# Row factors broadcast by way of DRAM, one gate behind a bank copy, and another order of VectorE's last steps

## The chip, the cores and the metric

The kernel runs on one core of a Trainium2 chip. Such a core has five engines with instruction queues of their own: TensorE (PE), which multiplies matrices; VectorE (DVE); ScalarE (ACT); GpSimd (POOL); and SyncE (SP), which here only issues transfers. Sixteen DMA engines move data between DRAM and the core's memory (SBUF); ACT, POOL and SP can issue transfers from their queues. PE writes its results to eight accumulation banks (PSUM) of 128 x 512 numbers of 32 bits, from which ACT and VectorE read them. Each engine works through its queue in order, and engines wait for one another through semaphores.

The metric is the device time of one execution in microseconds. The median of some runs is compared between two kernels; a profile comes from one more execution.

## The reference

One decoder layer on 1,024 tokens of width 1,024, in 32-bit floating point: a token mixer of two head groups (gated linear attention, GLA, and sliding-window attention), cross-attention into 256 memory tokens, and a gated MLP with a causal convolution of width 3. Each part begins with an RMS norm, and one more ends the layer.

```python
def rms_norm(x, g):
    xf = x.astype(jnp.float32)
    y = xf * lax.rsqrt(jnp.mean(xf * xf, axis=-1, keepdims=True) + EPS)
    return (y * g.astype(jnp.float32)).astype(x.dtype)

def conv_ffn(h, w_up, conv_w, conv_b, w_down):
    u = h @ w_up
    u = lax.conv_general_dilated(u, conv_w[:, None, :].astype(u.dtype), window_strides=(1,),
                                 padding=[(CONV_WIDTH - 1, 0)],
                                 dimension_numbers=('NWC', 'WIO', 'NWC'),
                                 feature_group_count=2 * D_FF) + conv_b
    gate, val = jnp.split(u, 2, axis=-1)
    return (jax.nn.silu(gate) * val) @ w_down
...
        hn = rms_norm(h, norm_mix[l])
        proj = hn @ w_in[l]
        gq, gk, gv, gr, ga, sq, sk, sv = jnp.split(proj, split_at, axis=-1)
...
        h = h + conv_ffn(rms_norm(h, norm_ffn[l]), w_up[l], conv_w[l], conv_b[l], w_down[l])
    return rms_norm(h, norm_final)
```

`D_FF` is 2,816, so the up projection has 5,632 columns: 22 column blocks of 128 for the gate and 22 for the values.

## The kernel before

**Products.** Every operand of a large product is split into a high part in a rounded 32-bit format (`float32r`), made by ACT, and a low part, made by VectorE as source less high part (`split`, lines 106 to 116; weights by way of `load`, line 118, from a staging buffer `st` into `w`). One product is three matmuls: high by high, high by low, low by high (`mm3`, line 147). PE's time is mostly these matmuls of 128 x 128 by 128 x 512.

**Order of the work.** A planner takes the program as written, models the time of each instruction, and fixes each engine's queue before the kernel runs. Inside `manual_schedule` the named engines keep the order of the program text among the instructions written there; others may be placed between them. `issue_after` and `add_manual_dep` with `NoSync` add an edge that only fixes which of two instructions of one engine is issued first. Waits for data are added by the framework. A pool's tag with `bufs=n` is a ring of n buffers; the banks are such rings too (`F`, `S`, `O`, `T`).

**The first stage, rows_a (line 467).** Eight row tiles of `x` (128 tokens each) are loaded. For each, PE transposes it (line 520), ACT and VectorE split the transposed tile into `xh` and `xl`, and PE multiplies it with 272 columns of `w_in`. PE, VectorE and ACT are in manual order. After each odd row tile, `factors` makes the sums of squares of two tiles on ACT (line 197) and their factors 1/rms by steps of two columns on ACT and VectorE (lines 183 to 191), into two columns of `rstd`, tile `rstd_x`, [128, 8]. `evac` scales the two results with them: `ga` on ACT (line 477), then two results on VectorE (line 479), of which `sv` goes to DRAM by POOL (`sv_d`, line 481) after every fourth tile.

Later products have the tokens along the free axis, so they need the factors as a row that stands in all 128 partitions: `rstd_bc`, tile `rbx`, [128, 1024]. `broadcast_rows` (line 199) makes it: for each half four matmuls of 128 columns of the factors, stretched along the free axis, by the identity (line 205; each shows as two instructions), into a bank of role `O`, and a copy by ACT (line 207). The call stands behind the manual block, so the planner places it.

**What follows it.** `vectors` brings gains into columns, by a transpose on PE; `swa_bias` makes the masks of the sliding window by way of two DRAM tiles (`line`, `skew`); `gla_gates` transposes `ga` (tile `prob`, line 676). `cols_swa` makes `sk` and then four tiles `sq`: for each half of the tokens 24 matmuls into one of the two `F` banks, and VectorE's `self.column` (line 610) multiplies bank and `rbx`. `save_x` writes `x` back to DRAM by VectorE sums (line 438) and POOL's queue (`xt_d`, line 439). Then the softmax of the sliding window runs on VectorE and ACT beside the column products of GLA on PE (`swa`, line 1008).

**The up projection (lines 1765 to 1904).** Column block j of the gate and block j of the values make a pair. Pairs 0 and 1 are done plainly (`up_plain`). Pair 2 is `up_first` and the others are `up_winograd`: seven block products `p1`, `p4`, `p6`, `p7` and so on instead of eight, with sums of weights (`t1` to `t4`, made by VectorE) and of activations (`s1` to `s4`); VectorE and ACT add the banks together. In `up_first`, `p5` is one of three `F` banks: the product of `t1` and `s1` is copied by ACT to `s5` (line 1853, tile `o`), and then PE adds the product of `b22` and `s4` to the same bank, so PE must wait for the copy.

`ffn_up(j)` (line 1896) finishes a pair: `conv` for both halves (one step on ACT, line 1890, and two on VectorE, line 1892, each), the Silu of the gate on ACT (line 1901), the product on VectorE (line 1902), and the write to DRAM by POOL. In `run`, `ffn_up(1)` stands between the parts of `up_first` (line 2288), and the code behind it is the second half of `up_first`.

**The end (lines 2163 to 2201).** The last product of the down projection ends with row tile 3 in manual order: its 512 columns come in two halves of 256 in two banks (`last_half`, line 2163). For each half VectorE adds the bank to `c12[3]` (line 2172), and ACT sums the squares (line 197). From the sums come the row factors (`partly`, line 2045; `guess`, lines 2048 to 2051; `newton`, lines 2055 and 2059), and `finish` scales two halves of the row tile: `one` on ACT (line 2065), `two` on VectorE (line 2070), each with a write to the output. Tile 2's `two` (`rows[i - 1][1]`) stands between the two halves of tile 3.

Of the kernel before, what the change touches and what calls it, by code (L numbers as in the profile page):

```python
# [28 lines left out]
P = 128  # L29
# [32 lines left out]
class Layer:  # L62
# [404 lines left out]
    def rows_a(self, keep, new):  # L467
# [40 lines left out]
        ssq = self.small("ssq", [P, NT], bufs=1)  # L508
        self.rstd = self.const.tile([P, NT], F32, name="rstd_x")
        self.rstd_bc = self.bc_tile("rbx")  # L510
        xh, xl = (self.xnew("x" + s, (P, NK, T), F32R) for s in "hl")
        self.x = [(xh[:, k], xl[:, k]) for k in range(NK)]
        self.xact = self.whole(self.x)
# [20 lines left out]
        with self.tc.manual_schedule(engines={e.PE, e.DVE, e.Activation}):  # L534
            transposed(0, 0)
            split_weights(st[0], 0, 3)
            transposed(0, 4)
            for i in range(NT):
                ps = self.bank("FO"[i % 2])
                cuts = (0, 3, 6, NK) if i == 0 else (0, NK)  # L540
                for k0, k1 in zip(cuts, cuts[1:]):
                    if i == 0 and k0:
                        split_weights(st[k0 // 3], k0, k1)
                    if i < NT - 1 and k1 == cuts[-1 if i == 0 else 1]:
                        transposed(i + 1, 0)
                        transposed(i + 1, 4)
                    products(ps, i, range(k0, k1))
                if i % 2:
                    for q in (i - 1, i):
                        factors(q)  # L550
                    evac(i - 1, done)
                    evac(i, ps)
                done = ps
        self.broadcast_rows(self.rstd, self.rstd_bc)

    def rows_b(self, new, weights, between):

# [1273 lines left out]
    def up_first(self, weights, new):  # L1831
# [18 lines left out]
        tt(out=u3, in0=p7, in1=u2, op=ALU.add)  # L1850
        tt(out=ug[:, t1s], in0=p4, in1=u3, op=ALU.subtract)
        product(p5, t1, s1, True)
        nc.scalar.copy(out=s5, in_=p5)  # L1853
        tt(out=uv[:, t1s], in0=s5, in1=u3, op=ALU.add)
        product(p5, b22, s4, False)
        tt(out=uv[:, t0], in0=p5, in1=u2, op=ALU.add)
# [39 lines left out]
    def ffn_up(self, j, us, new):  # L1896
# [1 line left out]
        nc = self.nc  # L1898
        yg = self.conv(us[0], j, new)
        yv = self.conv(us[1], NJ + j, new)  # L1900
        last = nc.scalar.activation(out=yg, in_=yg, func=AF.Silu)
        self.gated = nc.vector.tensor_tensor(out=yg, in0=yg, in1=yv, op=ALU.mult)
        nc.gpsimd.dma_start(out=self.g_d[j], in_=yg)
        return last
# [38 lines left out]
    def ffn_down(self, pre, hcnew):  # L1943
# [232 lines left out]
        def end(bank, ops):  # L2176
            with self.tc.manual_schedule(engines={mybir.EngineType.PE, mybir.EngineType.DVE,
# [7 lines left out]
                for i in range(4):  # L2185
                    _, (_, guess, newton, *partly) = factors[i]
                    if i < 3:
                        half_row(y[i], c12[i], i, 1)()
                    else:
                        read[0]()  # L2190
                    if i:
                        rows[i - 1][1]()
                    if i == 3:
                        partly[0]()
                        read[1]()
                    guess()
                    newton()
                    rows[i][0]()
# [134 lines left out]
```

## Time and profile before

| | us |
|---|---|
| median of 3 runs | 1272.4 |
| lowest and highest run | 1268.08, 1274.22 |
| the profiled execution | 1267.25 |
| its span, first to last instruction | 1265.5 |

The profile shows the profiled execution. In the timeline each row has the start in us from the span's start, the time, the engine, the line of the kernel, the operation, the tiles written and read (numbers of buffers left out), how many instructions were merged, and in brackets the idle time of the engine ahead of it and what ended that. `SPq`, `ACTq` and `POOLq` are queues that issue transfers. Matmuls are pipelined and their ends are modelled, so the distance from one start to the next says more than a duration. Some tiles carry the name of the buffer that they share: the second half of `up_first` writes into tiles called `o` and `uy`.

```profile
q1 hardware_dynamic: 173750, 121.51, 32.3%
q0 software_dynamic: 17184, 52.08, 12.7%
q10 hardware_dynamic: 160, 0.27, 0.1%
L207 ACT COPY rbx<-psO x2: 581/586/590, 41.9 to 45.7; 128x512 f32<-128x512 f32 x2
L191 DVE TENSOR_TENSOR rstd_x<-rs_y,rs_t x4: 151/160/161, 19.4 to 44.8; 128x2 f32<-128x2 f32 x4
```

The first three rows are DMA queues with packets, megabytes and the share of the sixteen engines' time: q1 is filled by SP, q0 by POOL, q10 by ACT. The last two are from the views of the tiles `rbx` and `rstd_x`: the shortest, median and longest time in ns, and the first and last start. The last factors are made at 44.8 us, and the second half of the broadcast row is copied at 45.7.

### The profile page before, as it was taken

The numbers are of one execution on the slowest core, as the hardware profiler recorded it, in microseconds if no ns is written. First come the engines' busy times: TensorE is split into PE (matmuls) and PEld (weight loads), VectorE is DVE, ScalarE is ACT, GpSimd is POOL, SyncE is SP. The second block draws the span as 40 slices with busy tenths as digits, with TensorE's granted clock in tenths as the row PEclk, the third lists the DMA queues.
The fourth block names the chain that finished last, engine by engine and source line by source line (L and its number), as shares of the span: only waits on it lengthen the run. The fifth ranks groups of instructions, "written<-read, shape, count | busy, mean of one in ns | idle before, by whom it ended". The sixth has DMA issues, their size and how long they took to land.

```text
span 1265.5 us, 19111 instructions
## 1 busy us (share of the span) xinstructions
PE 1249.9 (99%) x7303; PEld 1047.7 (83%) x7303; DVE 1005.9 (79%) x1697; ACT 632.2 (50%) x1167; POOL 124.4 (10%) x216
## 2 busy tenths in 40 slices
PE   8999999999999999999999999999999999999997
PEld 8887778989888889888887888888888888888886
DVE  6846886478556967897798989899888777999687
ACT  5426577246544535853566434434434435454455
POOL 1310332101221000000040000000000000000001
PEclk9999999999999999999999999999999999999999
DMA  7651355358643446153474335655622348610204
GB/s 229 201 154 51 85 135 139 121 183 272 208 150 115 139 150 223 44 180 129 141 133 126 100 109 141 150 124 140 185 83 68 100 149 326 227 64 10 74 24 152
DMA packets 191186, 175.08 MB, mean 138 GB/s; under 512 B 66689, under 2 KB 150838, under 8 KB 191094
## 3 DMA queue, kind: packets, MB, share of 16 engines
q1 hardware_dynamic: 173750, 121.51, 32.3%
q0 software_dynamic: 17184, 52.08, 12.7%
q8 instruction: 57, 0.93, 0.3%
q14 instruction: 35, 0.29, 0.1%
q10 hardware_dynamic: 160, 0.27, 0.1%
HBM read 121.64 MB, written 49.29 MB: 135 GB/s over the span
## 4 chain that ended last, share of the span: by engine, by line
PE 85%; DVE 8%; ACT 3%; DMA 2%; issue 1%; POOL 0%; SPq 0%; ACTq 0%; DVEq 0%; POOLq 0%
PE psS L1828 15%; PE psF L1828 14%; PE psF L1978 6%; PE psS L1978 6%; PE psF L1346 5%; PE psF L149 5%; PE psF L150 5%; PE psF L151 5%; PE psS L1623 3%; PE psO L1978 2%; PE psT L1978 2%; PE psS L149 2%; PE psS L150 2%; PE psS L151 2%; PE psF L1623 2%; ACT prob L1089 1%
## 5 line engine op out<-in xcount | busy, mean ns | idle before, releaser
L110 ACT CAST w<-st 128x1024 fp32r<-128x1024 f32 (+1 forms) x147 | 125.7, 858 | 187.4 <-PE psS L1978 39.9
L111 DVE TENSOR_TENSOR w<-st,w 128x1024 fp32r<-128x1024 f32 (+1 forms) x147 | 143.5, 978 | 48.9 <-ACT w L110 48.7
L1892 DVE SCALAR_TENSOR_TENSOR uy<-uy,vec,uy 128x1023 f32<-128x1023 f32 (+1 forms) x88 | 112.1, 1280 | 2.0 <-ACT uy L1890 0.4
L1828 PE MATMUL psS<-a,w 128*128 128x512 f32 x384 | 92.4, 389 | 0.0
L1978 PE MATMUL psF<-w,w 128*128 128x512 f32 x318 | 88.9, 389 | 0.0
L1978 PE MATMUL psS<-w,w 128*128 128x512 f32 x312 | 87.4, 389 | 0.0
L1828 PEld LDWEIGHTS psS<-a,w 128*128 128x128 f32 x384 | 72.1, 188 | 15.0
L149 PE MATMUL psF<-xh,w 128*128 128x512 f32 x208 | 83.1, 400 | 0.0
L150 PE MATMUL psF<-xl,w 128*128 128x512 f32 x208 | 81.6, 392 | 0.0
L151 PE MATMUL psF<-xh,w 128*128 128x512 f32 x208 | 81.2, 390 | 0.0
L1828 PE MATMUL psF<-a,w 128*128 128x512 f32 x336 | 80.7, 389 | 0.0
L1828 PEld LDWEIGHTS psF<-a,w 128*128 128x128 f32 x336 | 63.1, 188 | 13.1
L1978 PEld LDWEIGHTS psF<-w,w 128*128 128x128 f32 x318 | 59.7, 188 | 12.4
L1890 ACT ACTIVATE uy<-uy,vec 128x1024 f32<-128x1024 f32 x44 | 54.8, 1246 | 29.8 <-DVE uy L1883 26.5
L1978 PEld LDWEIGHTS psS<-w,w 128*128 128x128 f32 x312 | 58.6, 188 | 12.1
L1828 PE MATMUL psS<-act,wx 128*128 128x512 f32 x252 | 60.5, 389 | 0.0
L1828 PE MATMUL psF<-act,w 128*128 128x512 f32 x240 | 57.8, 390 | 1.4 <-ACT o L1853 1.4
L1828 PE MATMUL psS<-act,w 128*128 128x512 f32 x240 | 58.0, 389 | 0.0
L1828 PEld LDWEIGHTS psS<-act,wx 128*128 128x128 f32 x252 | 47.3, 188 | 9.8
L1089 ACT ACTIVATE prob<-prob,nm 128x256 f32<-128x256 f32 (+1 forms) x64 | 30.8, 482 | 48.6 <-DVE nm L1085 48.6
L1828 PE MATMUL psF<-act,wx 128*128 128x512 f32 x228 | 54.8, 389 | 0.0
L1828 PEld LDWEIGHTS psF<-act,w 128*128 128x128 f32 x240 | 45.0, 188 | 11.1 <-ACT o L1853 1.8
(582 smaller groups left out, 3101.1 us busy)
## 6 DMA issues: line engine op xcount, KB each, us to landing
st<-in_w_up_dram SPq DMA_DIRECT2D x44, 512.0 KB, 3.8
g_d<-uy POOLq DMA_DIRECT2D x22, 512.0 KB, 3.0
act<-in_w_down_dram SPq DMA_DIRECT2D x12, 512.0 KB, 9.1
st<-g_d SPq DMA_DIRECT2D x10, 512.0 KB, 3.2
res<-g_d SPq DMA_DIRECT2D x10, 512.0 KB, 10.7
st<-in_w_in_dram SPq DMA_DIRECT2D x9, 512.0 KB, 6.2
ow_d<-pts POOLq DMA_DIRECT2D x32, 128.0 KB, 3.5
st<-in_w_v_c_dram SPq DMA_DIRECT2D x8, 512.0 KB, 6.6
```

The source lines that it names most:

```text
L110: h = nc.scalar.copy(out=hi, in_=src)
L111: l = nc.vector.tensor_tensor(out=lo, in0=src, in1=hi.bitcast(F32), op=ALU.subtract)
L149: mm(out, lhsT=lh, rhs=rh, start=start, stop=False, skip_group_check=joined)
L150: mm(out, lhsT=lh, rhs=rl, start=False, stop=False, skip_group_check=joined)
L151: mm(out, lhsT=ll, rhs=rh, start=False, stop=stop, skip_group_check=joined)
L1089: last = nc.scalar.activation(out=prob[:, n, :nk], in_=prob[:, n, :nk], func=AF.Exp, bias=nm[:, n:n + 1], accum_out=den[:, n:n + 1])
L1346: mm(ps[n], lhsT=left[n][l][:, q], rhs=self.qa[right[n]][q][r], start=new and q == 0 and i == 0, stop=new and q == 3 and i == 2, skip_grou ...
L1623: mm(ps, lhsT=left[n][l][:, q], rhs=right[n][q][r], start=new and q == 0 and i == 0, stop=new and q == 3 and i == 2, skip_group_check=not new)
L1828: self.nc.tensor.matmul(ps, lhsT=b[l][:, q], rhs=a[q][r], start=first and q == 0 and n == 0, stop=first and q == 3 and n == 2, skip_group_ ...
L1890: nc.scalar.activation(out=y, in_=u, func=AF.Identity, scale=self.v("cw2", j), bias=self.v("conv_b", j))
L1892: nc.vector.scalar_tensor_tensor(out=y[:, s:], in0=u[:, :T - s], scalar=self.v(nm, j), in1=y[:, s:], op0=ALU.mult, op1=ALU.add)
L1978: nc.tensor.matmul(ps[i], lhsT=g[:, l, tk], rhs=w[:, r], start=first and k == 0 and m == 0, stop=first and k == n - 1 and m == 2, skip_gro ...
```

## The change

Three edits.

1. The call of `broadcast_rows` for the first factors is gone. After every fourth row tile, behind `evac` and inside the manual block, ACT's queue writes four columns of the factors to a small DRAM tile (`rstd_d`, in the order of the tokens), and POOL's queue reads the 512 numbers back into all 128 partitions of `rbx`. The other call of `broadcast_rows` stays.
2. In `up_first`, the copy of the bank to `s5` is to be issued on ACT ahead of the Silu that `ffn_up(1)` has written earlier. The edge sets an order on ACT and no wait.
3. At the end, the second half of row tile 3 is read from its bank, and its squares are summed, ahead of the scaling of row tile 2 on VectorE, and not behind it.

```diff
@@ -508,6 +508,7 @@
         ssq = self.small("ssq", [P, NT], bufs=1)
         self.rstd = self.const.tile([P, NT], F32, name="rstd_x")
         self.rstd_bc = self.bc_tile("rbx")
+        rstd_d = self.dram.tile([2, 4, P], F32, name="rstd_d")
         xh, xl = (self.xnew("x" + s, (P, NK, T), F32R) for s in "hl")
@@ -550,8 +551,12 @@
                         factors(q)
                     evac(i - 1, done)
                     evac(i, ps)
+                if i % 4 == 3:
+                    h = i // 4
+                    nc.scalar.dma_start(out=rstd_d[h].rearrange("i p -> p i"), in_=self.rstd[:, 4 * h:4 * h + 4])
+                    nc.gpsimd.dma_start(out=self.rstd_bc[:, 512 * h:512 * h + 512],
+                                        in_=rstd_d[h].rearrange("(o i) p -> o (i p)", o=1).to_broadcast([P, 512]))
                 done = ps
-        self.broadcast_rows(self.rstd, self.rstd_bc)
@@ -1850,7 +1855,10 @@
         product(p5, t1, s1, True)
-        nc.scalar.copy(out=s5, in_=p5)
+        read = nc.scalar.copy(out=s5, in_=p5)
+        self.tc.add_manual_dep(self.silu.ins, read.ins.name,
+                               mybir.DependencyInfo(mybir.DependencyClass.NoSync, mybir.DependencyReason.DATA),
+                               reason="the bank is read ahead of the gate")
         tt(out=uv[:, t1s], in0=s5, in1=u3, op=ALU.add)
@@ -1898,7 +1906,7 @@
-        last = nc.scalar.activation(out=yg, in_=yg, func=AF.Silu)
+        last = self.silu = nc.scalar.activation(out=yg, in_=yg, func=AF.Silu)
         self.gated = nc.vector.tensor_tensor(out=yg, in0=yg, in1=yv, op=ALU.mult)
@@ -2188,11 +2196,12 @@
                     else:
                         read[0]()
+                    if i == 3:
+                        read[1]()
                     if i:
                         rows[i - 1][1]()
                     if i == 3:
                         partly[0]()
-                        read[1]()
                     guess()
                     newton()
```

## The prediction

> **What bounds the kernel now.** I read the page's busy table first, then the busy time by stretch, then the DMA issues, and the timeline at the three places that the change touches.
>
> ```profile
> PE 1249.9 (99%) x7303; PEld 1047.7 (83%) x7303; DVE 1005.9 (79%) x1697; ACT 632.2 (50%) x1167; POOL 124.4 (10%) x216
> PE 85%; DVE 8%; ACT 3%; DMA 2%; issue 1%; POOL 0%; SPq 0%; ACTq 0%; DVEq 0%; POOLq 0%
> 128.00:160.00 32.00, 31.63 (x413) 24.82 (x402) 28.10 (x68) 18.87 (x53) 10.00 (x16) 1.00 0.35 85
> 690.00:705.00 15.00, 15.00 (x67) 12.41 (x67) 14.88 (x18) 7.18 (x9) 0.56 (x1) 1.00 0.41 125
> 1250.00:1265.50 15.50, 7.71 (x46) 6.69 (x44) 7.84 (x26) 7.60 (x22) 1.62 (x3) 0.90 0.36 135
> ```
>
> TensorE (PE) is busy for 99% of the span and makes 85% of the chain that ended last. In the rows of stretches the figures after the length are the busy time of PE, its weight loads, VectorE (DVE), ScalarE (ACT) and GpSimd (POOL). So a microsecond saved counts in full where it shortens PE's queue, or where it lies behind PE's last matmul, as in the last 15.5 us. It counts in part where another engine is as full as PE: VectorE has 14.88 of 15.00 us between 690 and 705, and 28.10 of 32.00 between 128 and 160. Each of the three edits falls under one of these.
>
> **Edit 1, the broadcast.** Before, PE copies the row factors to all partitions.
>
> ```profile
> 40.49 1.05 PE L205 MATMUL psO<-ident,rstd_x 128*128 128x128 f32 x8
> 41.30 0.48 PE L149 MATMUL psF<-xh,w 128*128 128x512 f32 x1
> ...
> 42.55 0.66 PE L205 MATMUL psO<-ident,rstd_x 128*128 128x128 f32 x4
> 42.97 0.48 PE L151 MATMUL psF<-xh,w 128*128 128x512 f32 x1
> 43.28 0.40 PE L149 MATMUL psF<-xh,w 128*128 128x512 f32 x1
> ...
> 44.98 0.71 PE L205 MATMUL psO<-ident,rstd_x 128*128 128x128 f32 x4
> 45.45 0.48 PE L150 MATMUL psF<-xl,w 128*128 128x512 f32 x1
> ```
>
> Durations overlap, so I count from start to start. The 16 instructions (two for each call) hold PE from 40.49 to 41.30, 42.55 to 42.97 and 44.98 to 45.45: 0.81 + 0.42 + 0.47 = 1.70 us. The first long matmul after a broadcast lasts 0.48 where the next lasts 0.40: 0.08 more, three times, 0.24. Removed from PE: 1.70 + 0.24 = 1.9 us. ACT also loses its two copies out of the bank, worth nothing, since PE doesn't wait for ACT in this stretch.
>
> Added are two DMAs per half of the rows: ACT's queue writes 512 numbers, each a piece of 4 bytes, and POOL's queue, which waits for that write, reads them back to all partitions (256 KB). The first half:
>
> ```profile
> 27.68 1.08 ACT L110 CAST xh<-psS 128x512 fp32r<-128x512 f32 x2
> 29.42 1.27 DVE L111 TENSOR_TENSOR xl<-psS,xh 128x512 fp32r<-128x512 f32 x2
> 50.15 0.68 DVE L610 SCALAR_TENSOR_TENSOR sk<-psF,rbx 128x512 f32<-128x512 f32 x1
> 1261.71 0.39 ACTq L2071 DMA_DIRECT2D out_dram<-c  x1
> ```
>
> ACT can issue its write at 27.68 and the factors are first used at 50.15: 22 us cover two DMAs. The issue (ACT's last one took 0.39) delays the casts queued behind it, but their reader on VectorE starts only at 29.42, so it hides. The second half is the tight one:
>
> ```profile
> 45.13 0.27 ACT L477 ACTIVATE ga<-psO,rstd_x 128x16 f32<-128x16 f32 x1
> 55.52 0.69 DVE L610 SCALAR_TENSOR_TENSOR sk<-psF,rbx 128x512 f32<-128x512 f32 x1
> 58.02 0.29 DVE L670 TENSOR_TENSOR prob<-ga,prob 128x128 fp32r<-128x128 f32 x1
> 59.34 1.03 PE L676 MATMUL psS<-ident,prob 128*96 128x128 f32 x8
> ke_d<-ke SPq DMA_DIRECT2D x8, 128.0 KB, 3.5
> mem_d<-st SPq DMA_DIRECT2D x8, 128.0 KB, 5.6
> res<-xt_d POOLq DMA_DIRECT2D x16, 256.0 KB, 3.2
> out_dram<-c SPq DMA_DIRECT2D x4, 256.0 KB, 2.2
> rel<-in_rel_bias_dram SPq DMA_DIRECT2D x1, 1.0 KB, 8.3
> 90.00:95.00 5.00, 5.00 (x24) 4.14 (x23) 0.69 (x1) 0.00 (x0) 0.00 (x0) 1.00 0.00 0
> ```
>
> The last figure of a DMA row is the time from issue to landing. ACT can issue behind `ga`, at 45.4. No row shows a write of 4-byte pieces; the bounds are the shortest and longest of these medians, 2.2 and 8.3, for each of the two DMAs in turn, so the second half is there between 45.4 + 4.4 = 49.8 and 45.4 + 16.6 = 62.0. I take the writes of 128-byte pieces, 3.5 to 5.6, middle 4.5, and the POOL read of the same size, 3.2: 53.1 us. When is that too late? PE would reach the end of `sk` at 55.5 - 1.9 = 53.6, so VectorE does not wait at all. If it waited, everything behind it would: from the second `sk` (55.52) to the end of `prob` (58.31) VectorE needs 2.8 us, and PE's transposes of `prob`, now due at 59.34 - 1.9 = 57.4, need that. So the limit is 57.4 - 2.8 = 54.6 us. With 53.1 the 1.9 us stay. Behind POOL's waiting DMA are the saves `xt_d`, `sv_d` and `line`. The longest chain from them leads over `line` to the masks of the softmax, and it has landed before 90: from there to 95 the DMA engines are empty (last row), and the scores come later still. That covers a delay of 5 us and more.
>
> The Trainium skill, "DMA: Bandwidth & Descriptors", section Specifications, says that pieces under 512 B make a DMA engine read, modify and write, which speaks against the 4-byte write; the same page, section Anatomy of one DMA, gives about 2.0 us plus bytes over 436 GB/s for each DMA. By that fit, an estimate, the pair would take 2.0 + 2.6 = 4.6 us and be there at 50.0, and the sum would be the same. No run here shows the 4-byte write.
>
> Does a saving at 45 us last? Up to 129 us the chain of work is PE. From 129 to 235 it is made of VectorE and ACT pieces, with PE filled by other products; those pieces start from PE's results at 129 and move with them. I let all of it pass, and keep 0 as the other end.
>
> **Edit 2, the gate.** The Silu of the second plain pair stands on ACT ahead of the copy for which PE waits.
>
> ```profile
> 679.05 2.88 PE L1828 MATMUL psF<-act,w 128*128 128x512 f32 x12
> 681.77 1.98 PE L1828 MATMUL psS<-a,w 128*128 128x512 f32 x8
> 685.16 3.01 PE L1828 MATMUL psF<-act,w 128*128 128x512 f32 x12 [1.42 <-ACT o L1853]
> 683.09 1.06 ACT L1901 ACTIVATE uy<-uy 128x1024 f32<-128x1024 f32 x1 [1.58 <-DVE uy L1892]
> 684.52 0.59 ACT L1853 COPY o<-psF 128x512 f32<-128x512 f32 x1
> 691.59 0.56 ACT L1871 COPY c<-psS 128x512 f32<-128x512 f32 x1
> 692.55 2.88 PE L1828 MATMUL psS<-a,w 128*128 128x512 f32 x12
> 695.30 0.68 DVE L1873 TENSOR_TENSOR c<-psS,c 128x512 f32<-128x512 f32 x1
> 696.63 2.88 PE L1828 MATMUL psS<-act,wx 128*128 128x512 f32 x12
> ```
>
> The bank is full at 679.05 + 2.88 = 681.93, ACT idles 1.58 us ahead of 683.09, and so the copy can end near 682.6 without holding up the Silu, which waits for VectorE anyway. PE's eight early matmuls end their turn at 681.77 + 8 x 0.227 = 683.58, and the next product starts there and not at 685.16: 1.6 us. What is late next? ACT's copy of the next pair ends at 692.15, and PE's use follows at 692.55, only 0.4 us later; VectorE's read of the next bank ends at 695.98, and PE overwrites at 696.63, 0.65 later. ACT and VectorE are tied to VectorE's full queue and don't come earlier by themselves. In the present order only 0.4 us would be left. But eight more matmuls of the pair's own `t1` product (1.8 us) wait behind these, and the planner fills such holes with them, as it did at 681.77. With all of them drawn ahead, the overwrite would be due at 696.63 + 0.45 - 1.6 = 695.5 (two of `t1` stand behind it now), so it starts at 695.98: 0.5 of the 1.6 lost, 1.1 left. I take 1.1; the ends are 0.4 and 1.6.
>
> **Edit 3, the end.** Nothing is added; one read moves ahead of a scaling.
>
> ```profile
> 1256.83 0.88 PE L2168 MATMUL psO<-pre,pre 128*128 128x256 f32 x6
> 1257.72 0.74 DVE L2070 SCALAR_TENSOR_TENSOR c<-c,ffac,nfin 128x512 f32<-128x512 f32 x1
> 1258.43 0.19 ACT L197 ACTIVATION_READ_ACCUMULATOR junk<-c 128x1 f32 x1
> 1258.73 0.42 DVE L2172 TENSOR_TENSOR c<-psO,c 128x256 f32<-128x256 f32 x1
> 1259.24 0.42 ACT L197 ACTIVATE junk<-c 128x256 bf16<-128x256 f32 x1 [0.62 <-DVE c L2172]
> ```
>
> PE's last matmul ends at 1257.71, so the second read can start at 1257.75 and not at 1258.73, and ends at 1258.17. Its sum of squares on ACT is then held by the first one, which ends at 1258.62; it starts at 1258.65 and not at 1259.24: 0.6 us. The scaling that moves back (0.74) ends near 1258.8, before the factors are needed (1259.2), and its output on POOL's queue leaves 0.4 us later, still far ahead of the last one. All that follows to the end hangs on this chain, so 0.6 us counts, between 0.5 and 0.6.
>
> **Sum.** 1.9 + 1.1 + 0.6 = 3.6 us, 0.3%. The profiled execution took 1267.25 us (span 1265.5), so it would become 1263.7. The median of the runs shown is 1272.4, 5 us above it, and its runs spread over 6 us; the forecast for the median is 1272.4 - 3.6 = 1268.8. About 0.5% (6.4 us) is what a measurement of this kernel can tell from no change.
>
> **Rivals.**
>
> First, *the first saving is lost*: the factors land near the point at which VectorE's wait eats it (54.6 + 1.9 = 56.5 us), or VectorE, 88% full between 128 and 160, holds PE there. For it: two DMAs in a row, and VectorE's fill. Against it: PE itself is busy for 31.63 of those 32 us. Left: 1.1 + 0.6 = 1.7; 1270.7.
>
> Second, *slower: the second half of the factors is late*. VectorE stands at `sk`, and the transposes of `prob` and all of PE behind them wait. Its price against before is the landing time less 56.5; it decides from there on, and at the upper bound of 62.0 it is 5.5. Less the 1.7 of the other edits: 3.8 slower, 1276.2. For it: writes of 4-byte pieces have no row, and the longest small DMA here took 8.3. Against it: that needs both DMAs at nearly the longest time.
>
> Third, *the gate's edge doesn't do what it says*: the copy still follows other ACT work, or the planner's new order gives back the 1.6. Then 1.9 + 0.6 = 2.5; 1269.9.
>
> **How the numbers follow.** Forecast 0.5, first rival 0.2, second 0.1, third 0.2. Forecast and rivals one and three all lie within 0.5%; only scatter of the medians, or a planner's order that happens to be much better, brings over 0.5%. Ends of the range: all ends at their best (1.9 + 1.6 + 0.6 = 4.1) against the lowest run, 1268.08, gives 1264.0; the highest run, 1274.22, with nothing gained, 1274.2. Chances: faster 0.15, within 0.5% 0.79, slower 0.06.
>
> **What would show it.** Right: no `L205` matmul on `rstd_x`; the second `sk` on VectorE near 53.6, with no wait for a DMA; the transposes of `prob` near 57.4; 129 to 235 passed 1.9 us earlier; no wait of PE for the copy into `o` at 685, and the next pair's work 2.5 to 3.5 us earlier in all at 705; 0.6 us less from PE's last matmul to the end. Wrong: a wait of VectorE on `rbx`, a new PE wait between 55 and 65 or 690 and 705, or another order of matmuls with waits of its own.

## The result, and the profile after

| | before | after |
|---|---|---|
| median, us (6 runs each) | 1268.17 | 1279.62 |
| lowest and highest run, us | 1267.64, 1274.22 | 1276.78, 1282.91 |
| profiled execution, us | 1267.25 | 1282.78 |
| its span, us | 1265.5 | 1281.1 |

The ratio is 1.008, with a 95% interval of 1.0051 to 1.0108: the changed kernel is slower by some 10 us (6.5 to 13.7; the two medians lie 11.5 apart), where the forecast said 3.6 us faster and the range ended at 1274.2. Three of the six runs before are those of the table ahead of the prediction; with the three others the median before fell from 1272.4 to 1268.17. From line 555 on, the lines of the changed kernel stand 5 lines further down than before, in the up projection and at the end up to 8.

The busy table and the chain of the changed kernel show hardly a difference:

```profile
PE 1254.8 (98%) x7287; PEld 1050.5 (82%) x7287; DVE 1006.2 (79%) x1697; ACT 631.5 (49%) x1165; POOL 125.7 (10%) x218
```

PE's sixteen broadcast instructions are gone (7303 became 7287), and yet PE is busy for 5 us longer, in a span that is 15.6 us longer. So PE both waits more and works more slowly. Its waits between 40 and 110 us say where (waiter, releaser, then the sum, the times and the longest, in us); before, this view shows no wait there:

```profile
PE psS L681 <- DVE prob L675: 4.8, 1, 4.8
PE psS L692 <- DVE prob L682: 2.6, 1, 2.6
PE psF L149 <- DVE sk L615: 1.3, 1, 1.3
```

All three hang on VectorE. VectorE's timeline in the same stretch shows what held it, and that it was not `rbx`; first a row of before, then rows of after:

```profile
47.20 1.21 DVE L123 TENSOR_TENSOR st<-st,vec 128x1024 f32<-128x1024 f32 x1
```

```profile
52.45 1.23 DVE L123 TENSOR_TENSOR st<-st,vec 128x1024 f32<-128x1024 f32 x1 [6.12 <-DMA st<-in_w_in_dram]
...
58.81 0.68 DVE L615 SCALAR_TENSOR_TENSOR sk<-psF,rbx 128x512 f32<-128x512 f32 x1
...
67.23 1.23 DVE L438 TENSOR_TENSOR gk<-xh,xl 128x1024 f32<-128x1024 f32 x1 [4.05 <-DMA xt_d<-gk]
```

VectorE waits 6.12 us for a load of weights that the change doesn't touch (before, the same instruction starts at 47.20 without a wait), and 4.05 us for a save (`xt_d`). The second product with `rbx`, at 58.81, waits for nothing. The DMA issues between 38 and 60 us, with the median time to landing at the end of each row, first before and then after:

```profile
st<-in_w_in_dram SPq DMA_DIRECT2D x4, 256.0 KB, 4.9
st<-in_w_in_dram SPq DMA_DIRECT2D x1, 512.0 KB, 7.4
```

```profile
st<-in_w_in_dram SPq DMA_DIRECT2D x4, 256.0 KB, 11.8
st<-in_w_in_dram SPq DMA_DIRECT2D x1, 512.0 KB, 12.5
rstd_d<-rstd_x ACTq DMA_DIRECT2D x1, 2.0 KB, 11.7
```

The new write of 2 KB lands after 11.7 us, and loads that share nothing with it but the DMA engines and DRAM take about twice their time. The stretches show the same from the side of the bytes (the last two figures are GB/s and, ahead of it, the time that packets took as a share of the sixteen engines' time, which here passes 1), again before and after:

```profile
46.00:50.00 4.00, 4.00 (x18) 2.27 (x16) 3.11 (x9) 0.32 (x1) 2.37 (x5) 1.00 1.22 277
```

```profile
46.00:50.00 4.00, 4.00 (x18) 3.29 (x18) 0.23 (x2) 0.00 (x0) 0.00 (x0) 1.00 2.16 69
62.00:66.00 4.00, 2.68 (x11) 2.34 (x11) 1.17 (x2) 0.00 (x0) 1.43 (x3) 0.50 0.96 366
66.00:70.00 4.00, 1.41 (x4) 0.80 (x3) 2.77 (x4) 0.00 (x0) 0.67 (x2) 0.50 0.28 109
70.00:75.00 5.00, 5.00 (x13) 3.85 (x13) 4.21 (x6) 4.95 (x10) 3.32 (x6) 0.50 0.75 286
75.00:80.00 5.00, 5.00 (x23) 4.07 (x22) 3.42 (x4) 2.03 (x4) 2.63 (x5) 0.94 0.42 145
```

Between 46 and 50 us the engines are busier and move a quarter of the bytes: 69 GB/s for 277. The column ahead of the DMA share is the clock that TensorE is granted: after the wait of 4.8 us it is 0.50 until 75 us, and PE works off in 70 to 75 us 13 matmuls, where it works off 23 in 75 to 80. At 100 us the changed kernel is 11.3 us behind (the first scores, line 1062 before, start at 100.94 and at 112.27).

GpSimd also waits, in its queue, for the write:

```profile
POOL rbx L557 <- DMA rstd_d<-rstd_x: 17.6, 2, 9.3
```

Behind its second wait stand the write of `line`, a memset, six small loads for `gla_gates` and the next saves, so this was a rival explanation. A third was the planner: an edit at one place can change its order at others.

### The profile page after: what moved, and what is told of

It is laid out like the page before. It is cut to its first block, busy times and chain, and to the rows that moved or that the text cites. A ratio compares the mean times of both kernels' runs of the same rounds, so it can differ in the third digit from the quotient of the medians.

```text
span 1281.1 us, 19082 instructions
## 1 busy us (share of the span) xinstructions
PE 1254.8 (98%) x7287; PEld 1050.5 (82%) x7287; DVE 1006.2 (79%) x1697; ACT 631.5 (49%) x1165; POOL 125.7 (10%) x218
## 4 chain that ended last, share of the span: by engine, by line
PE 82%; DVE 8%; DMA 4%; ACT 3%; issue 2%; POOL 0%; SPq 0%; POOLq 0%; DVEq 0%; ACTq 0%
PE psS L1833 15%; PE psF L1833 14%; PE psF L1986 6%; PE psS L1986 6%; PE psF L1351 5%; PE psF L149 5%; PE psF L150 5%; PE psF L151 5%; PE psS L1628 3%; PE psO L1986 2%; PE psT L1986 2%; PE psS L149 2%; PE psS L150 2%; PE psS L151 2%; PE psF L1628 1%
## 5 line engine op out<-in xcount | busy, mean ns | idle before, releaser
L1898 ACT ACTIVATE uy<-uy,vec 128x1024 f32<-128x1024 f32 x44 | 54.8, 1246 | 34.9 <-DVE uy L1891 26.9
```

The costliest lines, as they stand in the source:

```text
L1898: nc.scalar.activation(out=y, in_=u, func=AF.Identity, scale=self.v("cw2", j), bias=self.v("conv_b", j))
```

## Experiments

All times are medians in us; a ratio is against runs of the kernel before on the same chip, with its 95% interval. It is not the quotient of the two medians, and differs from that by up to 0.1%. An edit is against the kernel before, unless it says otherwise.

| kernel | median | before beside it | ratio | interval |
|---|---|---|---|---|
| only_broadcast | 1281.36 | 1268.51 | 1.0093 | 1.0076 to 1.0111 |
| write_only | 1278.55 | 1268.51 | 1.0083 | 1.0069 to 1.0097 |
| read_by_nobody | 1279.31 | 1268.51 | 1.0088 | 1.0074 to 1.0101 |
| gate_and_end | 1268.15 | 1268.51 | 0.9997 | 0.9986 to 1.0008 |
| write_only_16 | 1269.52 | 1269.86 | 1.0006 | 0.9991 to 1.0020 |
| wide_write | 1268.89 | 1269.86 | 0.9998 | 0.9985 to 1.0010 |
| first_half | 1269.40 | 1269.86 | 0.9992 | 0.9978 to 1.0006 |
| gate_held | 1272.38 | 1269.86 | 1.0014 | 1.0001 to 1.0026 |
| write_128_of_4 | 1277.89 | 1268.76 | 1.0072 | 1.0054 to 1.0090 |
| write_512_of_16 | 1268.36 | 1268.76 | 1.0007 | 0.9994 to 1.0020 |
| wide_first_and_end | 1270.08 | 1268.76 | 1.0004 | 0.9994 to 1.0015 |
| write_4_apart_512 | 1269.94 | 1270.31 | 1.0000 | 0.9988 to 1.0013 |
| write_4_apart_16 | 1268.61 | 1270.31 | 0.9997 | 0.9981 to 1.0013 |
| write_128_of_8 | 1269.27 | 1270.31 | 0.9990 | 0.9980 to 1.0000 |
| broadcast_16_and_end | 1274.26 | 1271.15 | 1.0028 | 1.0015 to 1.0041 |

### Which edit, and which half of it

*only_broadcast* is the changed kernel with edits 2 and 3 undone; *gate_and_end* is the changed kernel with edit 1 undone.

> Edit 1 alone, without the gate's edge and without the other end. If the whole loss is edit 1's, this is slower than the kernel before by 12 to 14 us (the 11.5 us of the whole change, and the 0.6 us of the end and up to 1 us of the gate that the changed kernel's trace shows as gained). If the gate's edge or another order elsewhere (the stall of 3.6 us on gvb near 250 us) is the cause of part of it, this is slower by less than 9 us.

> The whole change without edit 1. If edit 1 carries the loss and the two others keep what the changed kernel's trace shows, this is faster than the kernel before by 0.6 us (the end alone, if the gate's gain is lost again before 721 us) to 1.7 us (both as forecast). If the gate's edge does harm, it is slower than the kernel before.

Edit 1 alone is slower at a ratio of 1.0093; the two others alone are within 0.14% of the kernel before, so the 0.6 to 1.7 us that I expected of them can be neither seen nor excluded. The whole loss is edit 1's.

*write_only* keeps TensorE's broadcast and adds only the write of edit 1, which nobody reads:

```diff
+                if i % 4 == 3:
+                    h = i // 4
+                    nc.scalar.dma_start(out=rstd_d[h].rearrange("i p -> p i"), in_=self.rstd[:, 4 * h:4 * h + 4])
                 done = ps
         self.broadcast_rows(self.rstd, self.rstd_bc)
```

> The kernel before with the two writes of 512 pieces of 4 B added; nobody reads them, and the factors come by TensorE as before. Theory 'pieces' (the small pieces fill the DMA engines and hold up the weight loads): the loads of st near 46 us still land in over 10 us instead of 5.6 to 6.2, VectorE waits for st at L123, and most of the loss is here, 6 us and more. Theory 'queue' (GpSimd waits for the write, and six small loads behind it come late): no GpSimd wait is left, so the loss is under 2 us. Theory 'late factors' (only the arrival of the second half counts): within 1 us of the kernel before.

*read_by_nobody* adds to that a read on GpSimd's queue, at the place of the changed kernel's (besides, the planner moves one of VectorE's sums and the write of `line`):

```diff
+                    nc.gpsimd.dma_start(out=unread[h], in_=rstd_d[h])
```

> As write_only, and GpSimd issues at the same place a read of each written half into a DRAM tile that nobody uses; the factors still come by TensorE. Theory 'queue': GpSimd stands about 9 us near 46 to 55 us, TensorE waits again some 4.8 us at L681 near 60 us, and the loss is 8 us or more above write_only. Theory 'pieces': no more than 2 us above write_only. Theory 'late factors': still within 1 us of the kernel before.

In write_only the planned order of all five engines is that of the kernel before, instruction for instruction, but for the two issues on ACT. So no planner's choice, no late `rbx` and no wait of GpSimd for the write itself is left, and the kernel is still slower, at 1.0083, some 10.5 us. VectorE's and then PE's longest wait in its trace, the one between 38 and 66, the other between 40 and 110 us:

```profile
DVE st L123 <- DMA st<-in_w_in_dram: 6.8, 1, 6.8
```

```profile
PE psS L680 <- DVE prob L674: 5.8, 1, 5.8
```

VectorE is 5.95 us behind the kernel before at the second `st` (50.82 before, 56.77 here) and 7.1 behind at the `sq` products (73.85, 80.95); at 219.60 it is 8.2 behind. The weights are not all that comes late. GpSimd's two saves of that moment land after 13.5 and 14.9 us (before 5.1 and 7.0), its queue stands 7.37 and 2.21 us for their landing, and its small loads are late with it. From ACT's timeline of write_only:

```profile
62.66 0.40 ACT L667 CAST prob<-prob 96x256 fp32r<-96x256 f32 x1 [7.33 <-DMA prob<-in_b_alpha_dram]
```

VectorE takes up that result at 63.17, when it has worked off its backlog of the late weights: two paths behind the slow write end almost together. That is what theory "pieces" expected, and nothing is left for "late factors". GpSimd's wait for the write adds little: in read_by_nobody PE's longest wait is 8.5 us instead of 5.8, but the median is only 0.8 us higher and the intervals overlap. So "queue" falls as the main cause.

The rest of the distance in the profiled executions arises near 240 us, where PE waits for `gvb` (line 569), 0.7 us before and 4.3 us here. *before_again*, the kernel before unchanged, asks whether that belongs to the change:

> The kernel before, unchanged: another profiled execution, for the wait of TensorE for gvb near 240 us, which is 0.7 us in the first profile of before and 1.6 and 3.0 us in two kernels whose order is the same up to there. Theory 'run to run' (that wait moves with the landing of la<-mem_d): it lies anywhere between 0.7 and 4 us here too. Rival 'the change' (the shift of 11 us or the added DMAs bring it): 0.7 us again.

It took 1266.52 us. The rows of that wait in before_again, gate_held (below; its order is that of before up to the up projection) and write_512_of_16 (below; as fast as before):

```profile
PE psF L149 <- DVE gvb L569: 1.6, 1, 1.6
```

```profile
PE psF L149 <- DVE gvb L569: 3.0, 1, 3.0
```

```profile
PE psF L149 <- DVE gvb L574: 4.2, 1, 4.2
```

The wait moves from 0.7 to 4.2 us among kernels whose work up to there is the same but for a harmless write. So a difference of some us there between two single profiles is mostly that of two executions, and I don't count it to the change. In the traces of before and write_only it goes along with the later start of the second `la<-mem_d` (6.1 and 8.1 us behind the first). The five kernels with the dear second write have 2.4 to 4.3 us there in their one profile each, the five other kernels that only add a write 1.5 to 4.2. So whether the slow kernels meet a long wait there more often stays open: it would explain the 2 us between the 8.2 us that the trace of write_only has lost by 220 us and the 10 of the medians.

### What about the write is dear

*write_only_16* lays the four factors of a partition side by side, so the same 2 KB are 128 pieces of 16 B. *write_128_of_4* writes only one column of factors. *write_512_of_16* writes 512 pieces of 16 B from a constant tile. All keep TensorE's broadcast, and the order of the other engines. Their writes, in this order:

```diff
+                    nc.scalar.dma_start(out=rstd_d[h].rearrange("i p -> (i p)").rearrange("(p i) -> p i", i=4), in_=self.rstd[:, 4 * h:4 * h + 4])
```

```diff
+                    nc.scalar.dma_start(out=rstd_d[h, 0:1].rearrange("i p -> p i"), in_=self.rstd[:, 4 * h:4 * h + 1])
```

```diff
+        rstd_d = self.dram.tile([2, 4, P, 4], F32, name="rstd_d")
+                    nc.scalar.dma_start(out=rstd_d[h].rearrange("i p r -> p i r"),
+                                        in_=self.ident[:, 0:16].rearrange("p (i r) -> p i r", r=4))
```

> As write_only, with the same 2 KB for each half laid down as 128 pieces of 16 B instead of 512 of 4 B; the order of every engine is that of write_only. Theory 'pieces': what is paid goes by the number of pieces, so the write lands in about 3 to 5 us instead of 11.7, the wait of VectorE for st at L123 falls below 2 us, and the time is within 2 us of the kernel before. Rival 'any write there' (a small write at this place disturbs the DMA queues whatever its pieces, or the DRAM tile moves other tiles to worse addresses): still slower by 8 us or more.

> As write_only, but only one of the four columns of factors is written: 128 pieces of 4 B, 512 B in all, where the slow write had 512 pieces of 4 B and the harmless one 128 pieces of 16 B. The order of every other engine is that of the kernel before. Theory 'count' (each piece has its price, whatever its size): as write_only_16, within 2 us of the kernel before. Rival 'size' (a piece of 4 B is dear and one of 16 B cheap): a quarter or more of write_only's 10 us stays, 2.5 us and up.

> As write_only, with 512 pieces of 16 B at the same two places (8 KB each, from a constant tile; nobody reads them). Theory 'count': the loads of st wait as in write_only and the time is 8 to 12 us above the kernel before, although four times the bytes go. Rival 'size': within 2 us of the kernel before.

I had expected the price to go by the number of pieces, and the first run seemed to say so. The two others say the opposite: 128 pieces of 4 B cost 1.0072, nearly as much as 512, and 512 pieces of 16 B, with four times the bytes, cost nothing that can be measured. The write in the DMA issues between 38 and 60 us of write_only_16, write_128_of_4 and write_512_of_16:

```profile
rstd_d<-rstd_x ACTq DMA_DIRECT2D x1, 2.0 KB, 4.9
```

```profile
st<-in_w_in_dram SPq DMA_DIRECT2D x1, 512.0 KB, 15.3
rstd_d<-rstd_x ACTq DMA_DIRECT2D x1, 0.5 KB, 10.4
```

```profile
st<-in_w_in_dram SPq DMA_DIRECT2D x1, 512.0 KB, 8.5
rstd_d<-ident ACTq DMA_DIRECT2D x1, 8.0 KB, 5.7
```

Half a kilobyte in pieces of 4 B lands after 10.4 us and pushes a load to 15.3 (before, that load took 7.4); eight kilobytes in pieces of 16 B land after 5.7. So theory "count" falls. Left were the size itself, and the neighbourhood: in the dear writes each piece of 4 B lies next to one from another partition. Three more kernels tell them apart: write_4_apart_512, write_4_apart_16 (the same line, with a DRAM tile of [2, 4, P, 4]) and write_128_of_8:

```diff
+        rstd_d = self.dram.tile([2, 4, P, 128], F32, name="rstd_d")
+                    nc.scalar.dma_start(out=rstd_d[h, :, :, 0].rearrange("i p -> p i"),
+                                        in_=self.rstd[:, 4 * h:4 * h + 4])
```

```diff
+        rstd_d = self.dram.tile([2, P, 2], F32, name="rstd_d")
+                    nc.scalar.dma_start(out=rstd_d[h], in_=self.rstd[:, 4 * h:4 * h + 2])
```

> As write_only (512 pieces of 4 B for each half, the order of every other engine that of the kernel before), but each piece lies 512 B from the next in DRAM. Theory 'size' (a piece of 4 B is dear by itself): 7 to 11 us above the kernel before, as write_only. Rival 'sharing' (neighbouring pieces that fall into one stretch of DRAM wait for each other): within 2 us of the kernel before.

> As write_4_apart_512 with 16 B between the starts of the pieces, so that as many pieces lie in a stretch of DRAM as in write_512_of_16. Theory 'size': 7 to 11 us above the kernel before. Rival 'sharing': between the two, under 5 us, since a quarter as many share a stretch as in write_only.

> 128 pieces of 8 B, side by side, where 128 of 4 B cost 9 us. If what is dear is 4 B alone, within 2 us of the kernel before; if the price falls with the size, between 2 and 8 us above it; if it ends only at 16 B, 7 us and more.

All three are at 1.0000, 0.9997 and 0.9990 of the kernel before, with 1 within or at the edge of each interval. The write in the issues of write_4_apart_16 and of write_128_of_8:

```profile
rstd_d<-rstd_x ACTq DMA_DIRECT2D x1, 2.0 KB, 5.4
```

```profile
rstd_d<-rstd_x ACTq DMA_DIRECT2D x1, 1.0 KB, 5.8
```

The same 512 pieces of 4 B, 16 B apart instead of 4, cost nothing. So theory "size" falls too: pieces of 4 B are dear only where they lie side by side, and pieces of 8 B side by side cost nothing in the time. Their trace lies between, though: the load of 512 KB took 9.9 us in write_128_of_8, 8.1 in write_only_16 and 15.3 in write_128_of_4. So the effect may fade with the size of the pieces rather than end at 8 B. What in the DMA engines or in DRAM makes it so, no run shows.

Does it matter where the write stands? *first_half* sends only the first half of the factors through DRAM, in the dear form, at 26.9 us:

```diff
+                if i == 3:
+                    h = i // 4
...
                 done = ps
+        self.broadcast_rows(self.rstd, self.rstd_bc, (1,))
```

> Edit 1 for the first half of the factors alone (512 pieces at 26.8 us); the second half comes by TensorE as before. If only the second write's place hurts (at 42.5 us it meets the weight loads that are needed at 46 us), the time is within 1 us of the kernel before. If the first write takes as much, slower by 4 us and more.

At 0.9992 it costs nothing in the median, though GpSimd waits for it as long as in the changed kernel:

```profile
38.45 0.57 POOL L557 DMA_DIRECT2D rbx<-rstd_d  x1 [8.61 <-DMA rstd_d<-rstd_x]
```

The write was issued at 26.85, so it held the read back to 11.6 us behind its issue, in a stretch where SP issues only one small DMA and GpSimd only one save. The write of 16 B pieces in broadcast_16_and_end (below), issued at 26.92, lets the same read start at 29.90, at most 3.0 us later. So the dear write is slow without much traffic beside it, and there is little here for it to hold up. The trace is not free of it all the same: the late read and two saves behind it (38.45, 39.13 and 39.81) fall together with SP's loads from 40.28 on, and VectorE's timeline of first_half has

```profile
53.19 1.23 DVE L123 TENSOR_TENSOR st<-st,vec 128x1024 f32<-128x1024 f32 x1 [3.58 <-DMA st<-in_w_in_dram]
```

PE then waits 2.49 us at 61.66 for `prob`. What makes up for that in the medians I did not trace. TensorE also has eight broadcast instructions less here. As far as the medians go, the price is that of the second write, among the loads and saves that are issued from 40 us on; no run has the second write alone.

### Does the way through DRAM save anything without the dear write?

*wide_write* is edit 1 alone with the factors turned by TensorE into four rows, so that the write is four pieces of 512 B. *broadcast_16_and_end* is edit 1 with the layout of write_only_16, and edit 3; VectorE then reads `rbx` 16 B apart. *wide_first_and_end* takes wide_write's way for the first half alone, and edit 3.

The first two against edit 1:

```diff
+                    pt = self.bank("O")
+                    nc.tensor.transpose(pt[:4, :P], self.rstd[:, 4 * h:4 * h + 4], self.ident)
+                    line = self.rstd_bc[:4, 512 * h:512 * h + P]
+                    nc.scalar.copy(out=line, in_=pt[:4, :P])
+                    nc.scalar.dma_start(out=rstd_d[h], in_=line)
```

```diff
+        rstd_d = self.dram.tile([2, P, 4], F32, name="rstd_d")
+                    nc.scalar.dma_start(out=rstd_d[h], in_=self.rstd[:, 4 * h:4 * h + 4])
...
+                out=t[:, sl].rearrange("q (i p) -> q i p", i=4), in0=ps.rearrange("q (i p) -> q i p", i=4), scalar=scale,
+                in1=self.rstd_bc[:, sl].rearrange("q (p i) -> q i p", i=4), op0=ALU.mult, op1=ALU.mult)
```

> Edit 1 alone, but TensorE first turns the four columns of factors into four rows (one 128x4 transpose, one copy of 4x128 by ScalarE) and the write is four pieces of 512 B. Theory 'pieces': the write lands in 2 to 5 us, st loads in 5.6 to 6.5 us again, no TensorE wait near 60 us, and the time is from 1.5 us faster than the kernel before (the 1.9 us less the transposes) to 1 us slower. Rival 'GpSimd' (the read that waits on its queue is the cost): slower by 3 us and more even so, with the six small loads of L664 to L666 late and TensorE waiting at L681.

> Both halves of the factors through DRAM as in the changed kernel, but written as 128 pieces of 16 B, the four factors of a partition side by side; VectorE reads them in that order, 16 B apart, in its products with rbx. The new end is kept, the gate's edge is not. Theory 'pieces' with the prediction's first step: the write lands in about 5 us, the second half near 53 us, no wait for rbx and none at L681, and the time is 2 to 2.5 us below the kernel before (ratio 0.998). Rival 'late factors and queue': VectorE waits 1 to 3 us for rbx near 54 us as in wide_write, or TensorE for the gates' loads, and the time is that of the kernel before within 1 us. Third case: the read 16 B apart slows the products with rbx from 0.69 us, ten of them on VectorE near 54 to 80 us.

> The best that the runs point to: the first half of the factors through DRAM in four pieces of 512 B, the second by TensorE as before, the new order of VectorE's last steps, and no edge for the gate. About 0.8 us of TensorE's work and 0.6 us at the end are saved, the four transposed columns cost some 0.1 us: 1.3 us faster than the kernel before if nothing new waits (ratio 0.999), 0 if a wait takes the first part.

None is faster than the kernel before. wide_write is level (0.9998): its second write is issued only at 47.49 us, behind the transpose and the copy, and now the wait that I had named for the changed kernel is there. VectorE's timeline of wide_write:

```profile
57.34 0.69 DVE L619 SCALAR_TENSOR_TENSOR sk<-psF,rbx 128x512 f32<-128x512 f32 x1 [2.49 <-DMA rbx<-rstd_d]
```

broadcast_16_and_end is the form of which I expected 2 us. Here are the second read of its timeline, the second `sk`, the transposes of `prob`, and from the view of the tile `rbx` the longest group of products (shortest, median and longest time in ns):

```profile
47.49 0.55 POOL L557 DMA_DIRECT2D rbx<-rstd_d  x1 [1.85 <-DMA rstd_d<-rstd_x]
53.31 1.09 DVE L615 SCALAR_TENSOR_TENSOR sk<-psF,rbx 128x512 f32<-128x512 f32 x1
57.60 1.05 PE L682 MATMUL psS<-ident,prob 128*96 128x128 f32 x8 [0.52 <-DVE prob L676]
```

```profile
L615 DVE SCALAR_TENSOR_TENSOR gr<-psF,rbx x8: 1027/1086/1123, 176.0 to 225.5; 128x512 f32<-128x512 f32 x8
```

The factors are there at 47.49 + 4.8 (the landing of that read) = 52.3, and `sk` does not wait. The transposes of `prob` start at 57.60 instead of 59.34. The lead is then lost in two steps. The first is GpSimd's queue; rows of VectorE's and of PE's timeline:

```profile
58.49 1.23 DVE L438 TENSOR_TENSOR gk<-xh,xl 128x1024 f32<-128x1024 f32 x1 [1.04 <-DMA xt_d<-gk]
60.37 0.50 PE L693 MATMUL psS<-prob,prob 96*128 96x512 f32 x1 [1.00 <-DVE prob L683]
```

The save for which VectorE waits was issued at 52.86, behind the read of the factors, the write of `line` and the six loads; its sum was ready at 49.99. PE's wait of 1.00 us hangs on VectorE's. At the first scores, at 100.51, this execution is 0.43 us ahead of before, no more than it had been at 13 us. The second step is the reading 16 B apart: each of the 26 products with `rbx` takes 1.03 to 1.12 instead of 0.65 to 0.69 us, 10.2 us more on VectorE in all, and at the last of them it is 2.0 us behind (225.47, before 223.48). That is the third case of its expectation, and 1.0028 in time. What the 1.9 us would bring with products at their old speed was not tried; it would need the 16 B write and factors in plain order in SBUF, and the wait of 1.0 us suggests that half of the 1.9 would be lost even so.

wide_first_and_end, meant as the best, is level at 1.0004. So no version beat the kernel before by anything that can be measured.

### The gate

In gate_and_end the Silu stands behind the copies, as wanted, and PE waits as long as before. Rows of PE's and ACT's timelines of gate_and_end:

```profile
683.13 1.07 PE L1828 MATMUL psS<-a,w 128*128 128x512 f32 x4
685.67 3.06 PE L1828 MATMUL psF<-act,w 128*128 128x512 f32 x12 [1.47 <-ACT o L1853]
688.57 1.98 PE L1828 MATMUL psS<-a,w 128*128 128x512 f32 x8
```

```profile
684.55 0.58 ACT L1845 COPY uy<-psS 128x512 f32<-128x512 f32 x1 [1.58 <-DVE uy L1895]
685.03 0.59 ACT L1853 COPY o<-psF 128x512 f32<-128x512 f32 x1
685.50 1.07 ACT L1904 ACTIVATE uy<-uy 128x1024 f32<-128x1024 f32 x1
```

Before, eight matmuls stood ahead of the wait and four behind; now four ahead and eight behind. Besides, the copy into `o` stands on ACT behind another copy, and that one waits for VectorE (1.58 us), as the Silu did. *gate_held* adds an edge that keeps eight ahead (`held` is the first of the twelve matmuls that wait, the other the eighth of the next pair's first product):

```diff
+            self.tc.add_manual_dep(self.held.ins, self.blocks[-5].ins.name,
+                                   mybir.DependencyInfo(mybir.DependencyClass.NoSync, mybir.DependencyReason.DATA),
+                                   reason="eight of the next pair's matmuls ahead of the bank that is read")
```

> The gate and the end, with one more edge: the twelve matmuls that wait for the copied bank stand behind eight of the next pair's, as in the kernel before, not behind four. Theory 'given back' (the bank is read about 1 us earlier, but four of the eight matmuls that filled the wait were put behind it): the TensorE wait on o falls from 1.4 to about 0.5 us, and TensorE stands 0.9 us earlier after that group than in gate_and_end; in the time 0.5 to 1 us, which its measurement hardly tells. Rival (the bank is read no earlier): the wait grows no smaller than 1.4 us less the 0.9 us of the four matmuls in another place, and nothing is gained in the sum.

PE's timeline of gate_held:

```profile
685.88 1.98 PE L1828 MATMUL psS<-a,w 128*128 128x512 f32 x8
687.98 3.02 PE L1828 MATMUL psF<-act,w 128*128 128x512 f32 x12
...
698.74 3.65 PE L1828 MATMUL psS<-a,w 128*128 128x512 f32 x8 [2.76 <-ACT c L1881]
```

The wait for `o` is gone, and measured from 640 us PE is 1.4 us earlier against gate_and_end at the next group (2.74 us apart at 640, 1.36 at 690.38). "Given back" holds. But then PE waits 2.76 us for a copy of the next pair, and the whole is 1.0014. Taking one wait away showed the next, and a larger one.

## Why the prediction was wrong

**Edit 1, the step that failed.** The sum takes 1.9 us off PE and sets nothing against it: what the new write does to the other transfers has no term, and no reason is given for leaving it out. The prediction asked when the factors land, who waits for them, and what is queued behind GpSimd's waiting DMA ("That covers a delay of 5 us and more"), and not what shares the DMA engines with the write. Before, the stretch from 46 to 50 us moved 277 GB/s; SP had issued its loads from 41.26 us on, and VectorE used them at 47.20 and 50.82. With the write the same stretch moved 69 GB/s, VectorE waited 6.12 us for the weights and PE 4.8 us for VectorE. The row that I quoted for cover (90 to 95 us, engines empty) is 45 us too late. write_only shows the price of the missing term by itself: 1.0069 to 1.0097, 8.8 to 12.3 us.

**Two further readings of edit 1 were wrong.** The landing: the prediction bounded the write by the landing of other DMAs, 2.2 to 8.3 us, and took 4.5; it took 11.7, and 10.4 with a quarter of the pieces. The second half came at 54.79 + 3.9 = 58.7 us, inside the bounds of 49.8 to 62.0 but behind the limit of 54.6. By the prediction's own arithmetic that alone would have cost 58.7 - 56.5 = 2.2 us against before. Its reader at 58.81 did not wait only because VectorE was late already. The cover: the list of what stands behind GpSimd's waiting DMA leaves out the six loads for `gla_gates`, and the saves on the list were not covered. In the changed kernel the sum that VectorE had ready at 55.48 was saved from 59.55 on, behind the read and the loads; VectorE waited 4.05 us for that save, and PE 2.6 us for VectorE. How much of the loss in the medians this is stays open: read_by_nobody and write_only are not told apart.

**What a small write costs.** Pieces of 16 B, of 8 B, and of 4 B set apart landed after 4.2 to 5.8 us beside the traffic of 42 to 51 us, without the waits of the dear ones; 4 B pieces side by side took 10.4 to 13.3 us. The Trainium skill, "DMA: Bandwidth & Descriptors", section Specifications, says that pieces under 512 B make the engine read, modify and write. I named it against the write and gave it no price. All these pieces are under that threshold, so the threshold alone does not tell which of them are dear. The other figure of that page, 2.0 us and the bytes, in the section Anatomy of one DMA, is given there for transfers that GpSimd issues; I used it for the write too, which ACT issues. No write here whose landing is recorded took as little.

**PE's 1.9 us.** The matmuls are gone. In broadcast_16_and_end, where nothing is clogged, the transposes of `prob` start 1.74 us earlier, in an execution that stood 0.45 us earlier already at 13 us, and they wait another 0.52: 1.74 - 0.45 + 0.52 = 1.8. The size was right and the saving did not last: there PE lost 0.52 and 1.00 us in two waits for VectorE, the second by way of a save in GpSimd's queue.

**The landing by 53.1 us** was right for a write in whose place the 128 B writes may stand: with 16 B pieces, 52.3.

**The clock.** The prediction priced a wait by its length. A wait of 4.8 us also halved TensorE's clock: in the changed kernel it was 0.50 for 13 us (62 to 75). The Trainium skill, "TensorE: Matmul & The Clock Gate", section Part 1 (the HAM clock gate), says that an idle window of about 3.4 us brings the clock to half; the trace agrees with its 0.50 behind 4.8 us.

**Edit 2** was priced at 1.1 us and gave nothing (third rival: the planner's order gives it back). The step that failed is "the copy can end near 682.6": its neighbour on ACT waits for VectorE, so the copy started 4.62 us behind the start of the matmuls that fill its bank (680.41 to 685.03 in gate_and_end) and not 5.47 as before (679.05 to 684.52): 0.85 us earlier, not 2.5; and "the planner fills such holes" failed with it, since it drew four matmuls fewer, not more, ahead.

**Edit 3** was right. From the start of PE's last matmuls to the last issue on ACT's queue it was 1261.71 - 1256.83 = 4.88 us before, and in the timeline of the changed kernel

```profile
1273.08 0.88 PE L2176 MATMUL psO<-pre,pre 128*128 128x256 f32 x6
1277.37 0.36 ACTq L2079 DMA_DIRECT2D out_dram<-c  x1
```

4.29 us: 0.59 for a forecast of 0.6. All five kernels here with this edit have 4.29 in their profiles, the others 4.87 or 4.88. In the medians 0.6 us can't be seen.

**The rivals.** The second rival had the sign, at a chance of 0.1, but by the wrong way: it priced the factors' arrival at 5.5 us at most, and that arrival made nobody wait. So it is right in its direction by luck. The list "what would show it" named a new PE wait between 55 and 65, which came.

## What to carry to other kernels

Price a DMA not only by when it lands but by what else its engines have to move until then: look for the loads in flight at that moment and how soon they are wanted. A transfer from many partitions that sets pieces of 4 B side by side in DRAM is worth avoiding where other transfers are in flight, at 0.5 KB as at 2 KB; lay down at least 8 B per partition, or set the pieces 16 B apart. Where a queue will wait, list everything that stands behind the wait. And where a wait is taken away by an edge, see which matmuls the planner had put into it, and what the next wait is.

## What the runs showed that I had not expected

Pieces of 4 B are dear only side by side, and their number hardly matters: 512 B in 128 pieces of 4 B side by side land after 10.4 us and hold up a load of 512 KB to 15.3 us, while 8 KB in 512 pieces of 16 B land after 5.7 us and the load after 8.5. The queue of the write shows only a small share of the engines' time, and the loss stands in the other queues' rows; two of the three queues of write_only between 38 and 60 us (packets, MB, share; the third is q1, with 35.9%):

```profile
q0 software_dynamic: 609, 2.23, 63.4%
q10 hardware_dynamic: 528, 0.00, 1.6%
```

Before, q0 moved 3.74 MB there in 47.5% of the time. And VectorE products of 128x512 that read one operand 16 B apart took 1.03 to 1.12 us, for 0.65 to 0.69 in plain order.
